# Loading and rounding y of the first group ahead of x in a batched matmul on one Trainium2 core

One core of one Trainium2 chip. The metric is the device time of one execution in microseconds (us), the median of the runs quoted. The spans in the profiles are some 1.8 us shorter than these times.

## The reference

```python
batch, dim_i, dim_j, dim_k = 32, 256, 512, 384
# x: (32, 256, 512), y: (32, 512, 384), both float32
def reference(x, y):
    return np.einsum('bij,bjk->bik', x, y).astype(np.float32)
```

It reads 41.9 MB and writes 12.6 MB.

## The kernel before

The batch is worked in 8 groups of 4. A plan in text gives the order in which the parts of each group are issued: `x` and `y` load, `T` rounds x to 16 bits and transposes it (VectorE), `R` rounds y (VectorE), `M` multiplies (TensorE), `C` and `D` evacuate on ScalarE and VectorE, `S` stores. Below, x2 is x of group 2, and so on.

```python
PLAN = """
x0 x1 y0
T0 x2 y1
T1 R0 M0 C0 x3 y2
T2 D0 R1 M1 C1 x4 y3
...
"""
    x_pool = ctx.enter_context(tc.tile_pool(name="x_pool", bufs=2))
    y_pool = ctx.enter_context(tc.tile_pool(name="y_pool", bufs=2))
...
    def load_x(n):
        x_of[n] = x_pool.tile([P, R, J], F32, name="x_sb")
        keep(nc.sync.dma_start(out=x_of[n], in_=...))
...
    def transpose_x(n):
        x_r = xr_pool.tile([P, R, J], MM_DT, name="x_r")
        keep(nc.vector.tensor_copy(x_r, x_of.pop(n)))     # frees x's buffer
        ...
                keep(nc.vector.transpose(dst[:, c, e], src[:, c, e]))
```

There are two buffers for x, so the load of x2 can be issued only when x0 has been rounded. And all loads and stores go out in program order from one engine (SP), so whatever follows x2 in the plan waits behind it.

## Time and profile before

| | before |
|---|---|
| time, median of the first 3 runs (lowest to highest) | 134.30 us (134.27 to 134.54) |
| bytes moved | 54.5 MB, 410 GB/s over the span |
| busiest compute engines | VectorE 72%, ScalarE 69% |
| x2 issued at | 10.7 us |
| the first three loads have all landed at | 20.6 us |

The two busiest compute engines work for about 70% of the span. That alone does not tell what sets the time. In all views PE is TensorE, DVE VectorE, ACT ScalarE, and SPq the queue of SyncE; a line of a timeline begins with the start and the length of a piece, in us. A transfer has landed when the last of its 16 parts is reported complete.

### The profile page before, as it was taken

To read this page: it belongs to the slowest core of one execution; us is meant where nothing else is said; L and a number is where in the kernel's file an instruction comes from. 1 tells how busy PE (TensorE), PEld (TensorE's weight loads), DVE (VectorE), ACT (ScalarE), POOL (GpSimd) and SP (SyncE) were. 2 spreads that over 40 slices of the span, in tenths; PEclk is the share of its full clock that TensorE was granted. 3 is DMA by queue.
4 is the path that set the end of the run, shared out by engine and by line. 5 is a ranking of instruction groups with operands and counts; after the bars stand their busy time and mean duration, and the time that the engine had idled before them with its cause. 6 is when DMAs were issued, how large, how long until landed. Compare 5 with 4: busy or idle time off the path is not lost.

```text
span 132.9 us, 2437 instructions
## 1 busy us (share of the span) xinstructions
PE 61.5 (46%) x1024; PEld 34.9 (26%) x1024; DVE 96.1 (72%) x92; ACT 91.7 (69%) x193; POOL 0.2 (0%) x4
## 2 busy tenths in 40 slices
PE   0000004990399129924952395329540079887100
PEld 0000002550147014612541153115320034455000
DVE  0049999699959999999997999699951090735600
ACT  3000000089999999999999999999999961998500
POOL 0000000000000000000000000000000000000000
PEclk9999999999658975797799869985999555999955
DMA  4999999999999999999999999999999999999993
GB/s 109 429 424 441 451 414 429 446 429 412 419 471 407 404 437 441 432 409 446 429 417 414 456 432 402 414 419 429 429 464 429 414 451 400 419 425 412 400 412 141
DMA packets 3723, 54.68 MB, mean 412 GB/s; under 512 B 384, under 2 KB 384, under 8 KB 896
## 3 DMA queue, kind: packets, MB, share of 16 engines
q1 hardware_dynamic: 3712, 54.53, 96.9%
q8 instruction: 8, 0.13, 0.4%
q14 instruction: 3, 0.02, 0.0%
HBM read 41.94 MB, written 12.58 MB: 410 GB/s over the span
## 4 chain that ended last, share of the span: by engine, by line
DMA 45%; DVE 19%; ACT 15%; PE 10%; issue 4%; DVEq 1%
DMA x_sb<-in_x_dram 22%; DMA y_sb<-in_y_dram 22%; ACT o_sb L153 15%; PE o_ps L132 10%; DVE xt_sb L113 6%; DVE x_r L106 5%; DVE o_sb L153 4%; DVE y_r L119 4%; DVEq L202 1%; DVEq L106 0%
## 5 line engine op out<-in xcount | busy, mean ns | idle before, releaser
L153 ACT COPY o_sb<-o_ps 32x384 f32<-32x384 f32 (+1 forms) x192 | 90.4, 471 | 32.7 <-PE o_ps L132 25.8
L132 PE MATMUL o_ps<-y_r,xt_sb 32*128 32x384 f16 x1024 | 61.5, 399 | 61.7 <-DVE y_r L119 52.3
L132 PEld LDWEIGHTS <-xt_sb 32*128 32x128 f16 x1024 | 34.9, 113 | 87.9 <-DVE y_r L119 32.8
L119 DVE CAST y_r<-y_sb 128x1536 f16<-128x1536 f32 x32 | 28.5, 953 | 10.3 <-DMA y_sb<-in_y_dram 10.2
L113 DVE STREAM_TRANSPOSE xt_sb<-x_r 128x1024 f32<-128x1024 f32 (+1 forms) x20 | 31.7, 1631 | 0.3
L106 DVE CAST x_r<-x_sb 128x4096 f16<-128x4096 f32 x8 | 18.3, 2292 | 11.1 <-DMA x_sb<-in_x_dram 11.0
L153 DVE COPY o_sb<-o_ps 32x384 f32<-32x384 f32 (+1 forms) x32 | 17.8, 556 | 7.8 <-PE o_ps L132 3.8
L153 ACT ACT_TABLE_LOAD x1 | 1.3, 1283 | 0.7 <-PEq L191 0.7
L191 POOL MEMSET const-uint8-127<- 128x1 uint8 x1 | 0.1, 103 | 0.0
L191 POOL MEMSET const-bfloat16-1.0<- 128x1 bf16 x1 | 0.1, 102 | 0.0
L191 POOL MEMSET const-float32-0.0<- 128x1 f32 x1 | 0.1, 99 | 0.2 <-issue 0.2
L191 POOL MEMSET const-float32-1.0<- 128x1 f32 x1 | 0.1, 99 | 0.0
## 6 DMA issues: line engine op xcount, KB each, us to landing
y_sb<-in_y_dram SPq DMA_DIRECT2D x8, 3072.0 KB, 21.5
x_sb<-in_x_dram SPq DMA_DIRECT2D x8, 2048.0 KB, 22.0
out_dram<-o_sb SPq DMA_DIRECT2D x8, 1536.0 KB, 25.6
```

Of the source, the lines that this page charges most:

```text
L106: keep(nc.vector.tensor_copy(x_r, x_of.pop(n)))
L113: keep(nc.vector.transpose(dst[:, c, e], src[:, c, e]))
L119: keep(nc.vector.tensor_copy(yr_of[n][:, a : a + STEP], y_sb[:, a : a + STEP]))
L132: nc.tensor.matmul(ps_of[n, e, g], xt[s, e, t // 2, :, t % 2], y_r[s, t], start=(t == 0), stop=(t == T - 1),)
L153: keep(copy(o[a : a + w, g // per, h * NE + e], ps[h * w : (h + 1) * w]))
L191: nc = _bacc.Bacc("TRN2", target_bir_lowering=False, num_devices=1)
L202: with _tile.TileContext(nc) as tc:
```

## The change

y0 becomes the first load, and VectorE rounds it before it touches x0. The intent is to have the first matmuls start sooner: y0's rounding then fits in the wait for x0.

```diff
 PLAN = """
-x0 x1 y0
-T0 x2 y1
-T1 R0 M0 C0 x3 y2
+y0 x0 x1
+R0 T0 M0 C0 x2 y1
+T1 x3 y2
 T2 D0 R1 M1 C1 x4 y3
```

## The prediction

> **What bounds the kernel now.** I read four views in this order: the page's strip of forty slices, the table of stretches, the DMA queue's own timeline, and the chain that ended last.
>
> The strip first, because it shows at once which resource has no holes:
>
> ```profile
> DVE  0049999699959999999997999699951090735600
> ACT  3000000089999999999999999999999961998500
> ...
> DMA  4999999999999999999999999999999999999993
> GB/s 109 429 424 441 451 414 429 446 429 412 419 471 407 404 437 441 432 409 446 429 417 414 456 432 402 414 419 429 429 464 429 414 451 400 419 425 412 400 412 141
> ...
> q1 hardware_dynamic: 3712, 54.53, 96.9%
> ```
>
> Every slice of the DMA row but the first and the last is a 9, while VectorE and ScalarE have holes at both ends. The table of stretches gives the size of what is missing. Its columns are length; busy time and count of PE, weight loads, VectorE, ScalarE and GpSimd; granted clock; DMA share; GB/s:
>
> ```profile
> 0.00:2.00 2.00, 0.00 (x0) 0.00 (x0) 0.00 (x0) 1.27 (x1) 0.20 (x4) 1.00 0.44 82
> 2.00:4.00 2.00, 0.00 (x0) 0.00 (x0) 0.00 (x0) 0.01 (x1) 0.00 (x0) 1.00 0.69 229
> 4.00:12.00 8.00, 0.00 (x0) 0.00 (x0) 3.56 (x2) 0.00 (x0) 0.00 (x0) 1.00 1.01 432
> 12.00:17.00 5.00, 0.00 (x0) 0.10 (x1) 4.93 (x4) 0.00 (x0) 0.00 (x0) 1.00 1.01 436
> ...
> 20.70:34.40 13.70, 8.19 (x128) 4.54 (x127) 12.13 (x13) 7.09 (x16) 0.00 (x0) 1.00 1.01 431
> ...
> 66.00:99.00 33.00, 17.89 (x325) 10.44 (x318) 29.10 (x31) 31.99 (x69) 0.00 (x0) 0.90 1.00 424
> 99.00:126.00 27.00, 14.46 (x256) 7.96 (x256) 12.77 (x19) 20.71 (x44) 0.00 (x0) 0.81 1.00 423
> 126.00:130.40 4.40, 0.00 (x0) 0.00 (x0) 0.00 (x0) 0.00 (x0) 0.00 (x0) 0.56 0.97 405
> 130.40:132.90 2.50, 0.00 (x0) 0.00 (x0) 0.00 (x0) 0.00 (x0) 0.00 (x0) 0.50 0.12 49
> ```
>
> From 4 us to about 130 us the transfers run at 423 to 436 GB/s, share 1.0. The queue's 54.53 MB at 427 GB/s take 127.7 us. Add some 3 us lost in the first four (82 and 229 GB/s instead of 427) and some 2 us at the end when only stragglers move: 132.7, against a span of 132.9. The span is the stream of transfers plus its two ends.
>
> So the question is whether the change can leave that stream with nothing to do. For that I need when each transfer is issued and when it lands:
>
> ```profile
> 0.73 0.87 SPq L87 DMA_DIRECT2D x_sb<-in_x_dram  x2
> 1.65 0.42 SPq L96 DMA_DIRECT2D y_sb<-in_y_dram  x1
> 10.73 0.33 SPq L87 DMA_DIRECT2D x_sb<-in_x_dram  x1
> 11.10 0.43 SPq L96 DMA_DIRECT2D y_sb<-in_y_dram  x1
> 16.99 0.33 SPq L87 DMA_DIRECT2D x_sb<-in_x_dram  x1
> 24.36 0.33 SPq L96 DMA_DIRECT2D y_sb<-in_y_dram  x1
> ```
>
> Issue to landing, from the DMA view on narrow windows: x0 7.7, x1 12.1, y0 18.9, x2 14.7, y1 23.2, x3 22.2 us. So they land at 8.4, 13.3, 20.6, 25.4, 34.3 and 39.2. The steps of 4.9 us for 2.10 MB of x and 7.3 us for 3.15 MB of y are the 430 GB/s again; y1 took 1.5 us longer than its share. x2 is issued at 10.7, almost 10 us before y0 ahead of it is in. The queue is deep.
>
> Last, the chain, and why I don't take it at its word:
>
> ```profile
> DMA 45%; DVE 19%; ACT 15%; PE 10%; issue 4%; DVEq 1%
> ```
>
> It walks through DMA for under half of the span, because it goes from the last store to the last evacuation and back through compute. But the last store is issued at 125.6 and lands at 132.1, and the store ahead of it, issued at 120.5, lands 7.9 us later at 128.4: 2.8 us after the last issue. The last store queues behind bytes, so compute on that chain has slack.
>
> **What the Trainium skill says.** "DMA: Bandwidth & Descriptors", section Where 436 GB/s comes from, puts the ceiling of the 16 engines at 435 GB/s; the stretches above, 423 to 436, sit on it, so a full stream cannot be sped up by reordering. The same page, Queues, rings and completion order, says each engine consumes its descriptors in ring order; the landings agree (x0, x1, y0, x2, as issued), so I may shift them by bytes. "TensorE: Matmul & The Clock Gate", Part 1, gives half rate until about 3.4 us of activity; here the first 5.3 us of the first group (21.78 to the first evacuation at 27.09) hold half its matmuls and the remaining 2.9 us the other half, so I use 5.3 us for a cold first half.
>
> **The change part by part.** It adds and removes no instruction and no byte. Compared by engine, PE, ScalarE and GpSimd keep their order; VectorE moves four casts of y0 ahead of the first x, and SP issues y0 before x0 and x1 instead of after.
>
> *Loads.* All three are issued by about 2 us either way, and together end at 20.6 as before. y0 now lands first: 8.4 + (7.3 - 4.9) = 10.8. x0 at 15.7, x1 at 20.6.
>
> *VectorE.* Rounding y0 takes 3.54 us (four casts at 0.95, overlapped): 10.8 to 14.4. It then waits for x0 until 15.7. Cast of x0, 2.29: to 18.0. Two transposes, 3.9: to 21.9 (the first ends at 20.0). Cast of x1 to 24.2, transposes to 28.1. Before, both x were done at 20.9 and y0's casts at 24.3. The three jobs thus end 3.8 us later.
>
> *The refill of the queue.* Here is the only place where the stream can be hurt. x2 needs x0's buffer, free when x0 is cast: 18.0 instead of 10.7. The three first loads end at 20.6, and their fastest engines perhaps 0.6 us sooner. First packets need about 1 us after an issue (0.73, and bytes begin in the second microsecond). 18.0 + 1.0 = 19.0, ahead of 20.0 by about 1 us. So the margin falls from 9 us to some 1 to 2.5 us, but I expect no hole. y1 follows at once. x3 is issued at 24.2 (before 17.0), y2 right after at about 24.6 (before 24.4); the queue then holds work to 34.3. x4 at 30.4, y3 when y1 is rounded, 40.3 (before 37.9), with x4's landing at 51.4 ahead of it. Cost: 0, with a possible 0 to 1 us.
>
> *First matmuls.* y0 is rounded and the first half of x0's transposes ends at 20.0, so the first group starts 1.8 us earlier than 21.78. Evacuation starts about 20.0 + 5.3 = 25.3 instead of 27.09.
>
> *Second group.* VectorE reaches x2 at 28.1 instead of 25.6, ends it at 34.4, evacuates its four to 36.7, and rounds y1 from 36.7 instead of 34.35. The second group starts at 37.7 (35.37), and its first half ends near 43.0. ScalarE, which before worked from 27.09 to 108.6 without a pause (168 copies in 81.5 us, 28 copies or 13.6 us a group), now does 25.3 to 38.9, idles about 4 us, and runs five groups from 43.0 to 111.0. That is 2.4 us later than before. VectorE's own delay shrinks to about 1 us at the third x, whose landing (39.2) it awaits anyhow.
>
> *Does that reach the end?* Group 6 needs y6, which lands at 106.2 behind three stores (issued 76.6, 29.6 us). Its first half of banks is free at about 111.0 - 12 x 0.485 = 105.2, its second at 111.0, while its first half is multiplied until 112.6. Both are in time, by 1.0 and 1.6 us; ScalarE's hole of 4.0 us before 112.6 shrinks. From 106.2 on everything is as before. Store issues that move by 2.4 us have 10 us or more of queue ahead.
>
> Sum: bytes 0, refill 0 to +1 (expected +0.2), compute hidden both ways. 134.3 + 0.1 is my estimate: **134.4 us**.
>
> **The rivals.**
>
> (a) *The earlier start counts.* First matmuls 1.8 us sooner carry to the end: 132.5. For it: PE's largest wait is on VectorE's rounding, 52.3 us in 7, and the first group waited to 21.8. Against: no byte moves sooner, and every later group waits for its own load.
>
> (b) *The late x2 starves the queue.* A hole of 1 us, or 2 if the slow ramp of the first 4 us repeats: 135.3 to 136.3. For: the margin is 1 to 2.5 us, and the issue needs y0, its rounding, x0 and its cast in a row. Against: 18.0 is before 20.6 in any account, and the last store, issued 2.8 us before its predecessor landed, showed the rate holding at the end (405 GB/s from 126 to 130.4).
>
> (c) *ScalarE's 2.4 us survive.* If group 6's banks come late, the last store goes out at 128.0 instead of 125.6, and the end slips by at most 2.4: 136.7. For: the slack computed is only 1.0 to 1.6 us. Against: ScalarE's 4 us hole and the last store's 2.8 us of queue both have to be used up first.
>
> (d) *Luck among DMA engines.* y1's 1.5 us of excess looks like a straggler; if it lands on another or a second engine, the end moves by up to about 1 us either way.
>
> **Range and chances.** The centre is the unchanged stream. (d) and run scatter (134.27 to 134.54) give about half a microsecond each way; (b) and (c) stretch the upper side by one. Range 133.7 to 135.6. Two per cent is 2.7 us: faster would need bytes saved, and there are none, 0.01; slower would need (b) and (c) together, 0.03; the rest 0.96.
>
> **What would show it.** Right: DMA row of 9s throughout; y0 landing near 10.8; VectorE's first cast on y0, and its third block starting at x0's landing near 15.7; x2 issued near 18.0; no dip in GB/s from 18 to 21 beyond that of before; first matmul near 20.0; a new ScalarE hole of some 4 us near 39; y6 landing near 106. Wrong: a slice near 19 to 21 us at much under 400 GB/s would be (b); y6 at 106 but the last store issued after 127 would be (c); y6 and all later landings sooner by over a microsecond would refute the claim that bytes set the end.

## The result, and the profile after

| | before | changed |
|---|---|---|
| time, median of 6 (lowest to highest) | 134.34 us (134.27 to 134.54) | 136.12 us (134.99 to 136.82) |
| ratio, 95% interval | | 1.0127 (1.0084 to 1.017) |

A ratio here is the mean time of one kernel's fast runs over that of the other's of the same rounds, so not quite the ratio of the medians. The change costs 1.3%. That is less than the 2% from which the record calls a kernel slower, but the median lies outside the predicted range of 133.7 to 135.6, and the changed kernel scatters by 1.8 us where the kernel before scatters by 0.3.

The chain that ended last, by engine, in the changed kernel:

```profile
DMA 45%; DVE 19%; ACT 16%; PE 9%; issue 4%; DVEq 1%; SPq 0%
```

It hardly differs from that of before. Such shares do not show where 1.8 us came from. First, the issues of the DMA queue in order of time, and VectorE's first pieces:

```profile
0.73 0.39 SPq L96 DMA_DIRECT2D y_sb<-in_y_dram  x1
1.18 17.23 SPq L87 DMA_DIRECT2D x_sb<-in_x_dram  x3
18.45 0.43 SPq L96 DMA_DIRECT2D y_sb<-in_y_dram  x1
```

```profile
10.88 3.57 DVE L119 CAST y_r<-y_sb 128x1536 f16<-128x1536 f32 x4 [10.88 <-DMA y_sb<-in_y_dram]
15.75 2.30 DVE L106 CAST x_r<-x_sb 128x4096 f16<-128x4096 f32 x1 [1.30 <-DMA x_sb<-in_x_dram]
18.08 3.92 DVE L113 STREAM_TRANSPOSE xt_sb<-x_r 128x1024 f32<-128x1024 f32 x2
```

The second line of the first fence merges three loads of x: x0 and x1 at about 1.2 to 1.7 us, and x2, which ends that line, at 18.08 us. VectorE's lines say why: x0 lands at 15.7 us, its cast ends at 18.05 us, and only then is the buffer free. All this is as predicted. The strip of forty slices (3.37 us each) shows what came of it:

```profile
ACT  3000000799921999999999999999999990999500
...
DMA  5999989999999999999999999999999999999894
GB/s 131 438 428 428 428 375 336 435 406 423 418 452 445 411 433 443 414 426 431 438 418 440 426 431 406 382 418 423 452 438 428 438 416 423 420 417 392 369 392 168
```

Slices 6 and 7 (16.8 to 23.6 us) carry 375 and 336 GB/s where the kernel before carried 414 and 429. The DMA row shows it there as one lone 8 and would be easy to pass over. In stretches (columns as in the prediction; the last two are DMA share and GB/s), before and then changed:

```profile
19.00:20.70 1.70, 0.00 (x0) 0.00 (x0) 1.70 (x2) 0.00 (x0) 0.00 (x0) 1.00 0.79 337
20.70:23.00 2.30, 1.22 (x16) 0.66 (x19) 2.30 (x4) 0.00 (x0) 0.00 (x0) 1.00 1.06 456
23.00:26.00 3.00, 3.00 (x44) 1.68 (x40) 1.77 (x3) 0.00 (x0) 0.00 (x0) 1.00 1.06 453
```

```profile
19.00:20.70 1.70, 0.55 (x8) 0.29 (x12) 1.70 (x2) 0.00 (x0) 0.00 (x0) 1.00 0.64 241
20.70:23.00 2.30, 2.30 (x36) 1.15 (x32) 2.27 (x2) 0.00 (x0) 0.00 (x0) 1.00 1.03 378
23.00:26.00 3.00, 3.00 (x80) 1.81 (x76) 2.97 (x2) 1.70 (x4) 0.00 (x0) 1.00 0.95 388
```

From 19 to 26 us the kernel before moves 337 x 1.7 + 456 x 2.3 + 453 x 3.0 = 2.98 MB, the changed one 241 x 1.7 + 378 x 2.3 + 388 x 3.0 = 2.44 MB. The missing 0.54 MB are 1.26 us at 427 GB/s. Note the 337 in the row of before: in short stretches the figure jumps with how packets fall on the borders. To tell a true hole from that, I counted in the trace how many packets were under way at a time (there are 16 DMA engines, so 16 when all work; a 17 is two packets that overlap for some nanoseconds):

```
us            18.8 19.0 19.2 19.4 19.6 19.8 20.0 20.2 20.4 20.6 20.8 21.0 21.2 21.4 21.6 21.8
before          17   16   16   16   16   16   16   16   17   16   17   16   16   16   16   16
changed         17   16   16   14   11    8    9    9    9   11   11   12   13   14   16   16
```

Before, no engine is without work here. In the changed kernel the engines run out of x1 from 19.2 us on, about half of them get their first packet of x2 in time, and the rest only at 20.6 to 21.6 us, 2.5 to 3.5 us after the issue at 18.08. (The trace does not name the engine of a packet; this is read from the count.) Between 17 and 30 us an engine stands idle for 0.76 us on average, and for 0.00 before. On top, of 118 packets of 16 KB that started between 19.2 and 25 us, 45 took over 640 ns (up to 1318), where each of the 128 of before took at most 611.

How it reaches the end: each transfer's landing is counted by 16 increments, one for each engine. Over the 16, x2 landed at 24.9 to 25.5 us before and at 25.3 to 27.2 in the changed kernel. y6 landed at 104.1 to 106.2 before and 104.7 to 108.2 after; the last store at 132.05 before and 133.89 after. The loss of about 1.8 us of the slowest engine at 27 us is still there at the end. The last store is issued 2.05 us later (127.62 for 125.57), because y6, and with it everything of the last groups, came 2.05 us later.

ScalarE's evacuations in the changed kernel, for the rival that compute became late:

```profile
24.27 13.54 ACT L153 COPY o_sb<-o_ps 32x384 f32<-32x384 f32 x28 [22.26 <-PE o_ps L132]
43.25 67.80 ACT L153 COPY o_sb<-o_ps 32x384 f32<-32x384 f32 x140 [5.44 <-PE o_ps L132]
114.65 9.79 ACT L153 COPY o_sb<-o_ps 64x384 f32<-64x384 f32 x20 [3.60 <-issue]
```

ScalarE starts 2.8 us sooner than before, pauses 5.44 us, and ends group 5 at 111.05 instead of 108.6. It then still idles 3.6 us before group 6. So the delay is there, but has slack after it.

### The profile page after: what moved, and what is told of

It reads as the page before. It is cut to its first block, busy times and chain, and to the rows that moved or that the text cites. A ratio compares the mean times of both kernels' runs of the same rounds, so it can differ in the third digit from the quotient of the medians.

```text
span 134.7 us, 2436 instructions
## 1 busy us (share of the span) xinstructions
PE 59.7 (44%) x1024; PEld 32.5 (24%) x1024; DVE 96.2 (71%) x92; ACT 91.5 (68%) x193; POOL 0.2 (0%) x4
## 4 chain that ended last, share of the span: by engine, by line
DMA 45%; DVE 19%; ACT 16%; PE 9%; issue 4%; DVEq 1%; SPq 0%
DMA x_sb<-in_x_dram 23%; DMA y_sb<-in_y_dram 22%; ACT o_sb L153 16%; PE o_ps L132 9%; DVE xt_sb L113 6%; DVE x_r L106 5%; DVE o_sb L153 4%; DVE y_r L119 4%; DVEq L202 1%; SPq L96 0%; DVEq L106 0%
## 5 line engine op out<-in xcount | busy, mean ns | idle before, releaser
L132 PE MATMUL o_ps<-y_r,xt_sb 32*128 32x384 f16 x1024 | 59.7, 387 | 65.5 <-DVE y_r L119 34.8
L132 PEld LDWEIGHTS <-xt_sb 32*128 32x128 f16 x1024 | 32.5, 110 | 92.4 <-DVE y_r L119 37.1
L119 DVE CAST y_r<-y_sb 128x1536 f16<-128x1536 f32 x32 | 28.5, 955 | 20.3 <-DMA y_sb<-in_y_dram 20.2
## 6 DMA issues: line engine op xcount, KB each, us to landing
x_sb<-in_x_dram SPq DMA_DIRECT2D x8, 2048.0 KB, 20.5
```

Of the source, the lines that this page charges most:

```text
L119: keep(nc.vector.tensor_copy(yr_of[n][:, a : a + STEP], y_sb[:, a : a + STEP]))
L132: nc.tensor.matmul(ps_of[n, e, g], xt[s, e, t // 2, :, t % 2], y_r[s, t], start=(t == 0), stop=(t == T - 1),)
```

## The experiments

Three theories. A: x2 is issued so late that the DMA queue runs out of work on some or all engines, and a full stream never makes up for it. B: compute became late (VectorE's order, ScalarE's pause) and this reaches the end. C: y0 as the first load is in itself the dearer order. Each run's ratio is against runs of the kernel before in the same job, whose medians were 134.41 to 134.57 us.

**1. x2 with a buffer of its own.** It takes away what x2 waits for and leaves VectorE's order as changed. The space comes from the store side: that buffer later holds group 4's output, in place of a fifth output buffer.

```diff
-O_BUFS = 5
+O_BUFS = 4
...
+    own = own_pool.tile([P, R * J], F32, name="own_sb")
...
     def load_x(n):
+        if n == 2:
+            x_of[n] = own.rearrange("p (r j) -> p r j", r=R)
+        else: ...
...
     def multiply(n):
...
+        if n == 4:
+            o_of[n] = own[:, : R * K].rearrange("p (r k) -> p r k", r=R)
+        else: ...
```

> The changed kernel, but x of group 2 has a buffer of its own, so its load is issued at about 2 us instead of 18.1; VectorE's order is untouched. Theory A (the queue runs dry because x2 is issued 2.5 us before the queue's work ends): the hole at 19 to 22 us and the slow packets after it are gone, y6 lands near 106, time 134.3 (133.8 to 134.8). Theory B (compute that became late: ScalarE pauses 5.4 us before 43 us and ends group 5 2.4 us later): that pause stays, so the time stays near 136.1. Theory C (y0 first is itself the dearer order of loads): stays near 136.1.

Measured: 134.69 us, ratio 1.0014 (0.9995 to 1.0033). Its queue's issues, and the same stretches as above:

```profile
1.16 0.90 SPq L93 DMA_DIRECT2D x_sb<-in_x_dram  x2
2.10 0.65 SPq L93 DMA_DIRECT2D own_sb<-in_x_dram  x1
```

```profile
19.00:20.70 1.70, 0.29 (x4) 0.14 (x8) 1.70 (x2) 0.00 (x0) 0.00 (x0) 1.00 0.93 395
20.70:23.00 2.30, 2.30 (x36) 1.12 (x32) 2.27 (x2) 0.00 (x0) 0.00 (x0) 1.00 1.00 427
23.00:26.00 3.00, 3.00 (x80) 1.80 (x76) 2.97 (x2) 1.44 (x4) 0.00 (x0) 1.00 1.06 453
```

x2 goes out at 2.1 us, with y1 behind it at 2.8, the stretch carries 3.01 MB again, and no 16 KB packet between 19 and 45 us is slow. ScalarE's pause stays (5.42 us, resuming at 43.5). The time is that of before. So the late issue of x2 is the cause, and neither B nor C holds: VectorE's order, ScalarE's pause and y0 in front are all still in this kernel.

**2. Loads x0, y0, x1.** The diff is against the changed kernel.

```diff
-y0 x0 x1
-R0 T0 M0 C0 x2 y1
-T1 x3 y2
+x0 y0 x1
+T0 x2 y1
+R0 M0 C0 T1 x3 y2
```

> Loads in the order x0, y0, x1, and VectorE does x0, y0, x1: x0 lands at 8.4, x2 is issued near 10.7, y0 is rounded from 15.7, first matmul near 16.7. Theory A: no hole, 134.3. Theory B: the first matmul is 5 us sooner than before; if compute set the end, it would be faster, 130 to 133, or if ScalarE's pause of some 5 us before the second group (it resumes near 41.6) counts, 134.9. Theory C: no forecast.

Measured: 134.46 us, ratio 0.9989 (0.9969 to 1.001). x2 is issued at 10.85 us. ScalarE starts at 21.2 us, 5.9 us sooner than before, and pauses 6.7 us. Neither shows in the time: early compute buys nothing here, because the stream sets the end. In this trace the last of x2's 16 increments came at 27.14 us, as late as in the changed kernel (27.25), but it alone: the 15th came at 25.59. One engine that falls back by some 1.5 us is common to all the kernels (see the last section), and before it does so at y1. The landing of x2 by itself is therefore no measure of the hole.

**3. Only the loads of the change.** VectorE keeps the order of before, against which the diff is.

```diff
-x0 x1 y0
+y0 x0 x1
 T0 x2 y1
 T1 R0 M0 C0 x3 y2
```

> Only the loads of the change (y0, x0, x1); VectorE keeps the order of before (x0, x1, then y0). x0 still lands at 15.7 and x2 is still issued near 18.1, because y0's rounding fitted in the wait for x0. Theory A: the same hole as the changed kernel, 136.1, and up to 1.5 more because here ScalarE starts only near 34 and ends group 5 near 116, which is late for group 6: 136 to 137.5. Theory that the rounding ahead of x0 is what costs: back to 134.3.

Measured: 136.87 us, ratio 1.0173 (1.0152 to 1.0193). x2 is issued at 18.08 as in the changed kernel, and 8 of the engines stand idle from 19.8 to 20.6. The order of the loads, which puts x0 at 15.7 us, is thus enough for the hole; given these loads, the rounding of y0 ahead of x0 adds nothing to it. But this run has a second difference:

```profile
33.33 91.31 ACT L153 COPY o_sb<-o_ps 32x384 f32<-32x384 f32 x188 [31.32 <-PE o_ps L132]
```

ScalarE starts 9.1 us later than in the changed kernel and has no pause left. Its lateness opens no new hole up to y6 (from 30 to 105 us an engine idles for 0.03 us, as before), and y6 lands at 108.4 for 108.2. Whether the 0.75 us above the changed kernel's median is late compute or the scatter of another job was not tested.

**4. The changed kernel with x0 cast twice**, which holds x0's buffer 2.3 us longer and gives the same result.

```diff
+        if n == 0:
+            for _ in range(1):
+                keep(nc.vector.tensor_copy(x_r, x_of[n]))
         keep(nc.vector.tensor_copy(x_r, x_of.pop(n)))
```

> The changed kernel with the cast of x0 done twice, which holds x0's buffer 2.3 us longer: x2 is issued near 20.35 instead of 18.08, when the queue is all but empty. Theory A: the hole grows by nearly the whole 2.3 us, 138.0 to 138.6. Theory B: VectorE and ScalarE are 2.3 us later as well, and with 1.6 us of slack the end slips by under 1 us or not at all beyond what the loads do; x2 then y6 would land no later than in the changed kernel. Theory C: 136.1.

Measured: 137.51 us (136.67 to 137.66), ratio 1.0205 (1.0176 to 1.0234). It is slower than before, but by 1.4 us beyond the changed kernel and not by 2.0 to 2.5: the expectation was missed. More below.

**5 and 6. The same dose with the other order of loads.** On top of experiment 2, x0 is cast three times (`range(2)`) or four times (`range(3)`).

> Loads x0, y0, x1 as in the run with that order, and the cast of x0 done three times, so that x2 is issued near 15.3 instead of 10.7; the first three loads end at 20.7 as ever. Theory A: the changed kernel had its first packet of x2 1.3 us after the issue and the last of the 16 engines had its own 3.5 us after it; 15.3 + 3.5 = 18.8, before the first engine runs dry at 19.2: no hole, 134.5 (134.1 to 134.9). If the cost grew with any delay of x2, even one that leaves work in the queue, about 135.4.

> The same with the cast of x0 done four times: x2 issued near 17.6, 0.5 us sooner than in the changed kernel. Theory A: engines get work between 18.9 and 21.1 and run dry between 19.2 and 20, so a smaller hole than in the changed kernel: 134.8 to 135.8, between the two. Theory C (y0 first is what costs): 134.5, as y0 is second here.

Measured: three casts 134.30 us, ratio 0.999 (0.9967 to 1.0013); four casts 135.49 us (134.49 to 135.92), ratio 1.0066 (1.0034 to 1.0098). With three casts x2 is issued at 15.4 us and nothing is lost, though it is 4.6 us later than in experiment 2. With four it is issued at 17.9, and one engine or two of the 16 stand idle between 19.4 and 20.6. In its trace (a run of 135.81 us) one engine's part of x2 lands 1.3 us late, at 26.84. That does not show at once in the last landings, because another engine lags as much from y1 on in both (y1 lands at 34.16, and at 34.12 with three casts); from y5 on it does (72.30 for 70.69). Whether the lag of a single engine reaches the end thus seems to hang on which engines fall back later, which would fit the scatter of 134.49 to 135.92; no run tests it. So delay is free while enough is queued: an issue 5.2 us before the last landing of the work ahead lost nothing, one 2.9 us before it did. What lies between was not tried. C is excluded once more: y0 is second here, and the cost appears all the same.

**7. Only VectorE's part of the change.** The diff is against the kernel before.

```diff
 x0 x1 y0
-T0 x2 y1
-T1 R0 M0 C0 x3 y2
+R0 T0 M0 C0 x2 y1
+T1 x3 y2
```

> Only VectorE's part of the change: loads x0, x1, y0 as before, but y0 is rounded ahead of x0, so x0's buffer is held until y0 has landed at 20.6 and been rounded (24.2) and x0 cast: x2 issued near 26.5, 6 us after the queue is empty. Theory A: last engine of x2 restarts by about 28.7, x2 lands near 34 instead of 25.5, and the end moves by the same 8 to 8.5 us: 142 to 143.5. Theory B alone (lost compute, with its slack of about 1.6 us at the end and ScalarE's pauses): 6 us late first matmul, 138 to 140.

Measured: 143.36 us, ratio 1.0656 (1.0635 to 1.0677). Two of its stretches:

```profile
20.70:23.00 2.30, 0.00 (x0) 0.00 (x0) 2.30 (x3) 0.00 (x0) 0.00 (x0) 1.00 0.00 0
23.00:26.00 3.00, 0.00 (x0) 0.00 (x0) 3.00 (x3) 0.00 (x0) 0.00 (x0) 1.00 0.00 0
```

For these five microseconds not one byte moves. x2, issued at 26.44, lands at 34.2 instead of 25.5, 8.7 us later, and the time is 8.8 us above the job's median of before. The two halves of the change belong together: the rounding may come first only because y0 is loaded first.

**8. y1 ahead of x2.** y1's buffer is free from the start, so its load can fill the queue while x2 waits.

```diff
-y0 x0 x1
-R0 T0 M0 C0 x2 y1
-T1 x3 y2
-T2 D0 R1 M1 C1 x4 y3
+y0 x0 x1 y1
+R0 T0 M0 C0 x2
+T1 D0 R1 M1 C1 x3 y2
+T2 x4 y3
```

> The changed kernel with y1 (whose buffer is free) issued right after x1, so the queue holds work to about 28 when x2 is issued at 18.1; VectorE rounds y1 after the second x and takes the third x later, so ScalarE has no long pause. Theory A: no hole; 134.3 (134.0 to 134.8), with no gain over before, because no byte is saved and the stream sets the end. Theory B: ScalarE works from 24.3 on and would end group 5 near 106, so if compute set the end this would be the fastest, 132.5 or less.

Measured: 134.49 us, ratio 0.9999 (0.998 to 1.0018). x2 is issued at 18.2 us, later than in the changed kernel, and it costs nothing, because the queue holds 7 us more. No version tried beats the kernel before.

**9. Settling the miss of experiment 4.** The changed kernel again, experiment 4 again, and x0 cast three times.

> The changed kernel once more, beside the next two, because the run with x0 cast twice cost 1.4 us more than it and not the 2.0 to 2.5 expected. Expected: 135.5 to 136.8 again with its wide scatter, x2 issued near 18.1, GB/s falling to 200 to 300 between 19 and 20.7 us.

> x0 cast twice, the same kernel again: 137.2 to 137.8 if the miss was real, 138.0 to 138.6 if it was the chance of one job.

> x0 cast three times: x2 issued near 22.6, with every engine dry for over 2 us. If a delay counts in full once the queue is empty, this is 2.3 us above the kernel with two casts: 139.5 to 140.1. If late compute were what grows instead, the increase would differ from 2.3 and y6 would not land 2.3 us later.

Measured: the changed kernel 136.41 us (134.32 to 136.90); two casts 137.12 us (136.92 to 137.26), ratio 1.0199; three casts 139.39 us (139.32 to 139.51), ratio 1.0370. One of the six runs of the changed kernel took 134.32, so by the rule of 1.5% above the fastest four of the others count as slow and its ratio (1.0066) rests on two runs; the clocks of that fast run and of the slowest are alike (0.795 and 0.796). I take it as scatter of this kernel's own, and use only its range. The step from two casts to three is 2.27 us for an issue 2.64 us later, the order of size expected for a queue that is already empty (its time falls 0.1 us below the range given). The miss of experiment 4 was real. Engines with a packet under way, by time since x2's issue, show where it came from:

```
us after issue       0.0 0.4 0.8 1.0 1.2 1.4 1.6 1.8 2.0 2.4 2.8 3.2 3.6
changed, at 18.08     16  16  17  16  16  14   9   9   9   9  11  14  16
two casts, 20.24       0   0   0   4  11  12  13  13  15  15  16  16  16
three casts, 22.89     0   0   0   3  12  16  16  16  15  14  16  16  16
```

Issued on an empty queue, x2 reaches its first engine after 1.0 us and most within 1.4. Issued while x1 is still moving, half of the engines got work only after 2.5 us and more. The slowest engine of x2 therefore ended at 27.2 us in the changed kernel and at 27.9 with two casts: 0.7 us apart for 2.2 us of delay. Why the refill is slower on engines that are just running out is open; no run here separates it. Nor is it always so: the last store of the kernel before is issued at 125.57 us, just before the first engines run out of the store ahead. At 126.4 five engines are dry, and at 126.8, 1.2 us after the issue, all 16 have work.

All together, by the time of x2's issue (idle: mean of the 16 engines from 17 to 30 us, in the one profiled run of each):

| run | x2 issued, us | work queued ahead of it has landed, us | idle, us | median, us | ratio |
|---|---|---|---|---|---|
| own buffer | 2.1 | 20.9 | 0.00 | 134.69 | 1.0014 |
| before | 10.7 | 20.6 | 0.00 | 134.34 | 1 |
| x0, y0, x1 | 10.8 | 20.7 | 0.00 | 134.46 | 0.9989 |
| the same, 3 casts | 15.4 | 20.6 | 0.00 | 134.30 | 0.999 |
| the same, 4 casts | 17.9 | 20.8 | 0.10 | 135.49 | 1.0066 |
| changed | 18.1 | 20.6 | 0.76 | 136.12 | 1.0127 |
| loads only | 18.1 | 20.6 | 0.72 | 136.87 | 1.0173 |
| y1 ahead | 18.2 | 28.1 | 0.00 | 134.49 | 0.9999 |
| changed, 2 casts | 20.2 | 20.5 | 1.86 | 137.51 | 1.0205 |
| changed, 3 casts | 22.9 | 20.8 | 4.41 | 139.39 | 1.0370 |
| VectorE only | 26.4 | 20.6 | 7.85 | 143.36 | 1.0656 |

Every kernel without a hole takes the time of before, and every kernel with one takes longer, by the hole and another 0.6 to 1.6 us (medians against those of before in the same job). The slow first packets and the engine that restarts last are the likely rest; the parts were not separated.

## Why the prediction was right or wrong

*The stream sets the end: right.* Experiments 2 and 8 start ScalarE 5.9 and 2.2 us sooner and gain nothing; experiment 7 moves x2's landing by 8.7 us and the time by 8.8.

*Loads, VectorE and x2's issue: right.* y0, x0 and x1 were put at 10.8, 15.7 and 20.6 us and landed at 10.8, 15.7 and 20.6. x2's issue was put at 18.0 and came at 18.08; the first matmul at 20.0, and it came at 20.15.

*The refill of the queue: wrong, and this is the step that failed.* "18.0 + 1.0 = 19.0, ahead of 20.0 by about 1 us" has two terms that were mis-sized. The 1.0 us was read off the first packet at the kernel's start, and holds for the first packets on an empty queue (1.0 us in experiments 4 and 9). But a transfer has 16 engines, and here, with the queue nearly out, about half of them waited 2.5 to 3.5 us. The 20.0 was read off landings, which come after the data: packets end from 19.2 us on. The sum reads 18.1 + 3.5 = 21.6 against 19.2, a deficit of up to 2.4 us for the worst engine where I had written a margin of 1. The text gave this step "0 to +1 (expected +0.2)"; the whole change cost 1.8, and giving x2 its own buffer took all but 0.1 to 0.2 of it away.

*Rival (b) named this hole with 135.3 to 136.3 us*, which holds the measured 136.12, and even the repeated slow ramp was seen (45 slow packets). The argument against it, that "18.0 is before 20.6 in any account", compared an issue with a landing. The other, that the last store showed the rate holding, rested on a view that averages the 16 engines: five of them were dry at 126.4 us.

*ScalarE and rival (c): right.* Its restart was put at 43.0 and came at 43.25; its pause was put at 4 us and measured 5.44, because the first evacuation came at 24.27 and not at 25.3. The 5.3 us for a cold first half did not carry over: the first 64 matmuls took 4.8 us before and 3.8 here. They started 80 ns apart for the first 5.7 us before and for 2.7 here, and 40 ns apart after that. Over the 13 kept traces this step came after 2.7 to 5.7 us, on both sides of the 3.4 us that the prediction cites. The rest fits: group 5's end was put at 111.0 and came at 111.05. The pause costs nothing, as experiment 1 shows by keeping it.

*Rival (a): right to reject.* *Rival (d): in part.* One engine did lose 1.5 us at y1 in both kernels, so it is no difference between them. But the scatter of the changed kernel (134.3 to 136.9 over its 12 runs) was far larger than the half microsecond allowed for. Four casts, whose issue comes as close, scatter too (134.49 to 135.92). What differs from run to run is not shown: the two profiled runs of the changed kernel idle alike (0.76 and 0.74 us), and its fast run of 134.32 left no trace.

*A sum that is off:* the first four microseconds lose 2 x (1 - 82/427) + 2 x (1 - 229/427) = 2.5 us, not "some 3 us". Nothing hangs on it.

## What to carry to other kernels

Where transfers set the time, judge a reordering of loads by the issue that waits for a buffer: which load now frees that buffer later, and how much work the queue still holds at that moment. Count that margin to the first engine that goes dry, not to the last landing, and against the refill of all 16 engines; here an issue 2.9 us before the last landing ahead was already too late for an engine or two, and 5.2 us was early enough. If the margin is thin, put a load whose buffer is already free in between (experiment 8), rather than giving up the order.

## What the Trainium skill lacked or had wrong

- "DMA: Bandwidth & Descriptors", Latency and other measured facts, gives about 600 ns to the first byte for loads issued from SP. These runs agree if one counts from the end of the issue: 0.63 us on an empty queue, at the start of the changed kernel and for x2 in experiments 4, 7 and 9. The issue itself takes another 0.33 to 0.39 us, so that it is 1.0 us from its start. What no page tells is how the 16 engines follow: most within 1.4 us of the start on an empty queue, about half of them after 2.5 to 3.5 us when the queue was just running out.
- The same page's ceiling of 435 GB/s held (423 to 436 in full stretches), but no page warns that after a hole the first packets are slow: 45 of 118 took over 640 ns where 611 is normal.
- No page says how long the lag of one engine lasts: in experiment 2 the last increment of x2 came 1.55 us after the 15th, and three loads later, at y2, it was still 1.41 us behind (46.49 for 45.08).
- "Runtime: NRT & Kernel Launch", Instruction fetch mechanics, speaks of refills in 16 KiB blocks whose cost is mostly hidden. The trace agrees on their size (8 packets, 0.13 MB). But near the one at 30.5 us a single engine's share of y1 landed at 34.3 us, 1.5 us after the other 15, in the kernel before. The kept traces bear this out: the first such packet starts at 25.0 us in experiment 2 and at 36.9 in experiment 3, and there it is x2 and x3 whose one engine falls back by some 1.5 us. In each of the 13 traces the load under way at the first such packet takes the 16 engines together 1.3 us or more beyond its usual time. So the refill was not hidden for the engine that carried it. No run removes the packet.
